# Two blocks of a transformer on one core: the low part of the logits' moving side, on 64 rows and padded to 128

## The chip, the cores and the metric

The kernel runs as one program on one core of one Trainium2 chip. The metric is the device time of an execution in microseconds (us); the figure for a kernel is the median over its runs. Five engines of the core matter here: PE multiplies matrices (and loads the stationary side of each product, listed as PEld), DVE, ACT and POOL work on elements, and SP issues the transfers.

## The reference, cut to what matters

512 tokens of 1024 features pass through two layers of a first block and two layers of a second block, each block with a mixing part and feed-forward parts. The mixing parts hold the heads of 64 features that this case is about:

```python
# first block: 6 attention heads and 6 retention heads of 64 features
scores = jnp.einsum('bnqhd,bnkhd->bnhqk', q, kb)      # + relative bias, softmax, times V
sc     = jnp.einsum('bnihd,bnjhd->bnhij', qc, kc)     # retention: decayed, causal, no softmax
# second block: stick-breaking heads, and 6 sparse-attention heads with two branches each
z  = jnp.einsum('bqhd,bkhd->bhqk', qb, k) * scale     # stick-breaking, 4 heads
ss = jnp.einsum('bqgrd,bgqnld->bgrqnl', qb, kg)       # selected keys
sw = jnp.einsum('bqgrd,bkgd->bgrqk', qb, kwb)         # window keys
```

All of these are products over 64 features. A further kind of head in the second block (MLA) has products over 96 features and is not touched.

## The kernel before, in words

Every large product is made of float parts: a number is split into a high part (rounded to the fast matmul type) and a low part (the rest), and a product is taken as high times high, low times high and high times low. For weights this is three passes per block of 128 x 128 (lines 529 to 531), each with a stationary load and a moving side of up to 512 tokens. The whole kernel is a stream of such passes, fed by weights that SP loads, ACT rounds (line 511) and DVE subtracts (line 513).

For the logits of a 64-feature head the three products fit into two passes, since the array has 128 rows. The stationary tile `st` holds the high part of a head in 64 rows and its low part in the other 64 (`still`). The moving tile `mh` holds the high part in both halves, so the first pass (line 616) gives high times high and low times high at once. The second pass (line 617) adds stationary high times moving low: only 64 rows have something to add, and it uses 64 rows of the stationary tile and 64 rows of `ml`. One tile `ml` holds the low parts of both heads of a pair, each in its own half.

`movings` makes these tiles: ACT writes the high part into one half, ACT or DVE copies it into the other, DVE writes the low part. It is called for retention queries (`rq`) and attention keys (`ak`) in the first block, three pairs each, and for stick-breaking queries (two pairs) and the keys `ks` and `kw` in the second: 20 times in all over two layers of each block. `qk` is called four times per head and branch, on 128, 256, 384 and 512 columns (tiles of queries against the keys up to them, or the reverse): 56 heads and branches, so 224 calls. The softmax (lines 714 to 726), transposes (line 744) and the product with the values (`pv`, line 776, 64 columns of the array per head) follow.

The order of the work is set in two steps: hand-written lists of jobs (`ORDER1`, `ORDER2`, `LAGS`) interleave heads with projections, and a scheduler then orders the instructions of each engine and gives tiles slots from pools. The pool `s` has 50 slots of 128 x 512; `mh`, `ml` and `st` come from it. Each engine runs its list strictly in order.

Of the kernel before, what the change touches and what calls it, by code (L numbers as in the profile page):

```python
# [11 lines left out]
F32 = mybir.dt.float32  # L12
# [7 lines left out]
T = 512  # L20
# [23 lines left out]
# stages for which a job of a kind waits before its next one  # L44
# [5 lines left out]
# the engine of each kind of copy, by phase  # L50
# [5 lines left out]
# taps of the convolution between two stages of its job  # L56
CONV_STEP = 2
# tiles of the first products by halves of the tokens, in block 1's FFN and in the FFN that follows block 1
HEAD1 = 4
HEAD2 = 2  # L60
# how the end of a phase is woven into the next products
# [6 lines left out]
# ---------------------------------------------------------------- host layout  # L68
# [44 lines left out]
class Plan:  # L113
    """Weights in chunks of at most 1024 columns of 128 rows, and the order in which the program takes them."""
# [18 lines left out]
class Blank:  # L133
    """Stands for the program's objects where only the order of the weights is asked for."""
# [14 lines left out]
# the jobs of each kind, in their order  # L149
# [13 lines left out]
# the order of the jobs of the two mixing phases; each advances those ahead of it by a stage  # L163
# [132 lines left out]
def _bias_master(rel_bias):  # L296
    """[layer, head, 128 queries, 512 keys] of the last query tile; keys of a later chunk are masked."""
    p = np.arange(128)[:, None]
    c = np.arange(512)[None, :]
    idx = np.clip(p + 384 - c, -128, 128) + 128  # L300
    m = rel_bias[:, :, idx]
    m[:, :, np.broadcast_to((c >= 448) & (p < 64), idx.shape)] = NEG
    return np.ascontiguousarray(m.astype(np.float32, copy=False))
# [48 lines left out]
# ---------------------------------------------------------------- the program  # L352
# [3 lines left out]
class Normed:  # L356
    """An input that awaits its norm's factor: the gained input in two parts, and the factor once known, as a row on
    all partitions and by token."""
# [6 lines left out]
class Prog:  # L365
# [23 lines left out]
    def phase(self, name, **bufs):  # L389
        """Pools of one phase: slots of [128, 512], long tiles of [128, 1280], values by token."""  # L390
        es = ExitStack()
        self.pools = {t: es.enter_context(self.tc.tile_pool(name=self.nm(name + t), bufs=b)) for t, b in bufs.items()}
        return es
# [41 lines left out]
    def pf(self, w=512):  # L435
        """Banks of every kind in turn, where no attention runs."""
        turns = "".join(t * b for t, b in BANKS.items())
        self.turn = (self.turn + 1) % len(turns)
        return self.bank(turns[self.turn], w)

    # ---- constants
    def consts(self):
        nc, A = self.nc, self.A

        def c(nm, shape, dt=F32):
            return self.cst.tile(shape, dt, tag=nm, name=nm)

        self.ident = c("ident", [128, 128])
        make_identity(nc, self.ident)
        self.ones = {}  # L450
        for d in (1024, 256, 128):
            self.ones[d] = c(f"ones{d}", [128, 1])
            nc.vector.memset(self.ones[d], 1.0 / d)
        self.one1 = c("one1", [128, 1])
        nc.vector.memset(self.one1, 1.0)
        self.m256 = c("m256", [128, 128])
        nc.vector.memset(self.m256, 1.0 / 256)
        self.m64 = c("m64", [128, 128])
        nc.vector.memset(self.m64, 0.0)
        nc.vector.memset(self.m64[0:64, 0:64], 1.0 / 64)  # L460
        nc.vector.memset(self.m64[64:128, 64:128], 1.0 / 64)
        self.tri = c("tri", [128, 128], F32R)
        nc.gpsimd.memset(self.tri.bitcast(F32), -1.0)
        nc.gpsimd.affine_select(self.tri, self.tri, pattern=[[-1, 128]], compare_op=ALU.is_ge,
                                fill=0.0, base=0, channel_multiplier=1)
        self.neg1 = c("neg1", [128, 128], F32R)
        nc.gpsimd.memset(self.neg1.bitcast(F32), -1.0)
        self.identr = c("identr", [128, 128], F32R)
        nc.vector.tensor_copy(self.identr, self.ident)
        self.smask = c("smask", [128, 128], F32R)  # L470
        nc.gpsimd.memset(self.smask.bitcast(F32), NEG)
        nc.gpsimd.affine_select(self.smask, self.smask, pattern=[[-1, 128]], compare_op=ALU.is_ge,
                                fill=0.0, base=0, channel_multiplier=1)
        # the first use of ScalarE loads its table while the first transfers are under way
        nc.scalar.activation(c("warm", [128, 1]), self.one1, AF.Copy)
        self.vec = c("vec", [128, NVEC])
        nc.sync.dma_start(self.vec, A["vec"])
        self.cmpv = c("cmpv", [128, 4])
# [9 lines left out]
    # ---- weights  # L488
# [11 lines left out]
    def fetch(self, end):  # L500
        """Loads and splits the chunks of the sequence before the given place."""
# [36 lines left out]
    def lin_tok(self, name, l, hd, width, tt, banks, sink):  # L538
        """Products by token, for the 128-token tiles tt; returns what hands them on."""
        mm = self.nc.tensor.matmul  # L540
        ps = {t: b(width) for t, b in zip(tt, banks)}
        for k in range(KD):
            wh, wl = self.blk((name, l, k))
            for t in tt:
                s = slice(128 * t, 128 * t + 128)
                mm(ps[t], hd.hi[k][:, s], wh, start=k == 0, stop=False)
                mm(ps[t], hd.lo[k][:, s], wh, start=False, stop=False)
                mm(ps[t], hd.hi[k][:, s], wl, start=False, stop=k == KD - 1)
            self.step()

        def end():
            for t in tt:
                sink(t, ps[t], hd.rt[:, t:t + 1])
        return end
# [6 lines left out]
    def open_mix(self, tok, names, l, hd, sink, halves):  # L561
        """The first products of a mixing phase, if so by halves of the tokens: values by token, two linear tiles."""
# [22 lines left out]
    # ---- splitting  # L585
# [15 lines left out]
    def movings(self, src, scale=None):  # L601
        """For the moving side, of both 64-row halves: [hi; hi], and lo in the rows that hold it."""
        lo, out = self.R("ml"), []
        for half in range(2):
            a, b = slice(64 * half, 64 * half + 64), slice(64 - 64 * half, 128 - 64 * half)
            m = self.R("mh")
# [3 lines left out]
            out.append((m, lo, a))  # L610
        return out

    def qk(self, ps, st, mv, c, stop=True):
        """ps = the product of a stationary [hi; lo] tile's columns and a moving side's columns c."""
        m, lo, a = mv
        self.nc.tensor.matmul(ps, st, m[:, c], start=True, stop=False)
        self.nc.tensor.matmul(ps, st[a], lo[a, c], start=False, stop=stop)  # L617

    def still(self, src, half, scale=None):
        """[hi; lo] of 64 rows for the stationary side."""  # L620
# [6 lines left out]
    # ---- norms  # L627
    def rstd(self, pc, n):
        """(pc + eps) ** -0.5 on [128, n]: Newton's steps from an estimate by the exponent's bits."""
# [12 lines left out]
    def bcast_rows(self, y, nt, g, bank=None):  # L642
        """y [128 tokens, nt * g] to a PSUM tile [128 = (g rows), nt * 128 tokens]."""
# [11 lines left out]
    def mean_rstd(self, accs, d, t0=0, t1=512, bank=None):  # L655
        """The norm's factor by token from squares in one or more tiles."""
# [40 lines left out]
    # ---- softmax attention over keys <= the end of the query tile  # L697
    def softmax(self, scores, master, gate=None, negated=True):
        """scores(qt, ps) emits the products, of the negated logits if so; yields, then normalises and transposes."""
# [33 lines left out]
    def key_parts(self, t):  # L733
        """A long tile as four key tiles, each with the queries from its own on."""
# [15 lines left out]
    def pipeline(self, jobs):  # L750
        """Each job's first stage follows one stage more of each of the jobs under way."""
# [19 lines left out]
    def pv(self, po, v, o, pts, start=True, stop=True):  # L771
        """po[:, q] += V^T P^T of two heads side by side in the array; their values are columns o on of v."""
# [6 lines left out]
    # ---- block 1  # L779
# [180 lines left out]
    def tail(self, keys_of, rh, rl, sink, done, halves):  # L960
        """The last products of a phase, if so by halves of the tokens."""
# [11 lines left out]
    def step(self):  # L973
        """A stage more of the end of a phase, whose stages are woven into the next products."""
        next(self.pending, None)

    def drain(self):
        """The rest of these stages; the norm's factor, if any, then takes their place."""
# [4 lines left out]
    def post_norm1(self, xs, f, g_post, g_next):  # L983
        """The sink and the end of a tail in block 1, and the next input."""
# [59 lines left out]
    def ffn(self, parts, head, names, l, hd, evict, partial):  # L1044
        """Up and down products part by part, the first ones by halves; returns what the tail takes."""
# [74 lines left out]
    # ---- block 2  # L1120
# [165 lines left out]
    def misc(self, l, hd, cx):  # L1286
# [6 lines left out]
        # the rotated key that all heads share  # L1293
# [4 lines left out]
        # gates by token  # L1298
# [77 lines left out]
    def nsa_in(self, l, hd, nx, nm, p=None):  # L1376
        """A linear tile, rotated but for the compressed values."""
# [27 lines left out]
        else:  # L1405
            # [128 = (token, token + 16) of 64 features, part, group, token]; the positions' part in the last 16 columns
# [38 lines left out]
    def compressed(self, l, nx, nm):  # L1445
        """Compressed keys (for both sides of the split) or values (block-diagonal by group)."""
# [4 lines left out]
        if nm == "k":  # L1451
# [8 lines left out]
            # columns by group, part and block  # L1460
# [4 lines left out]
        else:  # L1465
            # [128 = (copy, group, block), 64]
# [13 lines left out]
    def compressed_attention(self, nx, cx):  # L1480
        """All heads of two query tiles at a time; columns by pair, group and block."""
# [129 lines left out]
```

## Time and profile before

| | |
|---|---|
| runs | 3394.7, 3396.48 and 3407.11 us, median 3396.48 |
| profiled execution | span 3401.8 us (the page gives no other time of it) |
| PE busy | 3329.6 us, 98% |
| DVE / ACT / POOL busy | 1948.0 (57%) / 1349.7 (40%) / 258.7 us (8%) |
| first block's mixing parts | about 50 to 250 us and 690 to 900 us |
| second block's mixing parts | about 1650 to 1950 us and 2700 to 3000 us |

The busy time of PE includes the time in which a matmul is still in the pipeline, so two matmuls that follow each other overlap in the list. What a pass costs the stream is read from the distance between its start and the start of the next one. A stationary load is listed under PEld with its own start.

### The profile page before, as it was taken

The numbers are of one execution on the slowest core, as the hardware profiler recorded it, in microseconds if no ns is written. First come the engines' busy times: TensorE is split into PE (matmuls) and PEld (weight loads), VectorE is DVE, ScalarE is ACT, GpSimd is POOL, SyncE is SP. The second block draws the span as 40 slices with busy tenths as digits, with TensorE's granted clock in tenths as the row PEclk, the third lists the DMA queues.
The fourth block names the chain that finished last, engine by engine and source line by source line (L and its number), as shares of the span: only waits on it lengthen the run. The fifth ranks groups of instructions, "written<-read, shape, count | busy, mean of one in ns | idle before, by whom it ended". The sixth has DMA issues, their size and how long they took to land. (4 is left out here: it accounts for less than half of the span.)

```text
span 3401.8 us, 41132 instructions
## 1 busy us (share of the span) xinstructions
PE 3329.6 (98%) x15956; PEld 2697.0 (79%) x15956; DVE 1948.0 (57%) x3381; ACT 1349.7 (40%) x2254; POOL 258.7 (8%) x301
## 2 busy tenths in 40 slices
PE   8999999899999999999999999999999999999998
PEld 6778888877888888888877578888888877678887
DVE  5967334778744457454677564545445468554454
ACT  4364323435543333232566632223222366642231
POOL 2102000220200020000200010001000120010001
PEclk9999999999999999999999999999999999999999
DMA  5222222332132222232333022222222323112222
GB/s 166 89 70 81 97 96 99 112 121 85 57 112 96 97 93 98 95 99 95 114 86 112 13 94 99 99 93 95 98 99 93 118 81 106 52 62 99 95 97 69
DMA packets 100867, 317.28 MB, mean 93 GB/s; under 512 B 12608, under 2 KB 18112, under 8 KB 100672
## 3 DMA queue, kind: packets, MB, share of 16 engines
q1 hardware_dynamic: 100672, 314.66, 28.0%
q8 instruction: 125, 2.05, 0.2%
q14 instruction: 70, 0.57, 0.1%
HBM read 298.75 MB, written 6.29 MB: 90 GB/s over the span
## 5 line engine op out<-in xcount | busy, mean ns | idle before, releaser
L511 ACT ACTIVATE wh<-raw 128x1024 fp32r<-128x1024 f32 (+2 forms) x546 | 567.8, 1041 | 1411.6 <-PE pd L530 618.6
L513 DVE TENSOR_TENSOR wl<-raw,wh 128x1024 fp32r<-128x1024 f32 (+2 forms) x546 | 663.0, 1216 | 440.5 <-ACT wh L511 439.0
L529 PE MATMUL pd<-hh,wh 128*128 128x512 f32 (+1 forms) x1328 | 509.7, 386 | 3.7 <-ACT wh L511 3.7
L530 PE MATMUL pd<-hl,wh 128*128 128x512 f32 (+1 forms) x1328 | 509.3, 384 | 3.3 <-DVE hl L681 3.1
L531 PE MATMUL pd<-hh,wl 128*128 128x512 f32 (+1 forms) x1328 | 508.9, 384 | 2.1 <-DVE wl L513 2.1
L676 POOL TENSOR_TENSOR acc<-acc,sq 128x256 f32<-128x256 f32 (+1 forms) x160 | 172.4, 1081 | 2195.9 <-ACT sq L675 2190.6
L529 PEld LDWEIGHTS pd<-hh,wh 128*128 128x128 f32 x1328 | 251.1, 190 | 56.9 <-issue 6.7
L530 PEld LDWEIGHTS pd<-hl,wh 128*128 128x128 f32 x1328 | 252.4, 190 | 51.6 <-DVE hl L681 4.9
L531 PEld LDWEIGHTS pd<-hh,wl 128*128 128x128 f32 x1328 | 252.1, 190 | 49.6 <-DVE wl L513 2.5
L530 PE MATMUL pt<-hl,wh 128*128 128x512 f32 x480 | 189.7, 396 | 8.2 <-DVE hl L681 8.2
L530 PE MATMUL ps<-hl,wh 128*128 128x512 f32 (+1 forms) x528 | 196.8, 373 | 0.0
L529 PE MATMUL ps<-hh,wh 128*128 128x512 f32 (+1 forms) x528 | 196.5, 372 | 0.0
L531 PE MATMUL ps<-hh,wl 128*128 128x512 f32 (+1 forms) x528 | 196.3, 373 | 0.0
L531 PE MATMUL pt<-hh,wl 128*128 128x512 f32 x480 | 189.2, 395 | 0.0
L529 PE MATMUL pt<-hh,wh 128*128 128x512 f32 x480 | 188.6, 394 | 0.0
L529 PE MATMUL pd<-ah,wh 128*128 128x512 f32 (+1 forms) x498 | 185.0, 372 | 0.0
L530 PE MATMUL pd<-al,wh 128*128 128x512 f32 (+1 forms) x498 | 184.8, 371 | 0.0
L531 PE MATMUL pd<-ah,wl 128*128 128x512 f32 (+1 forms) x498 | 184.8, 371 | 0.0
L720 ACT ACTIVATE P<-P,st 128x128 f32<-128x128 f32 x192 | 107.0, 558 | 54.7 <-DVE st L714 44.1
L587 ACT ACTIVATE ah<-sc 128x512 fp32r<-128x512 f32 x88 | 55.6, 632 | 183.7 <-DVE sc L1129 183.7
L529 PE MATMUL pt<-ah,wh 128*128 128x512 f32 (+1 forms) x332 | 123.5, 372 | 0.0
L530 PE MATMUL ps<-al,wh 128*128 128x512 f32 (+1 forms) x332 | 123.4, 372 | 0.0
(475 smaller groups left out, 6510.9 us busy)
## 6 DMA issues: line engine op xcount, KB each, us to landing
raw<-in_w SPq DMA_DIRECT2D x514, 512.0 KB
raw<-in_w SPq DMA_DIRECT2D x20, 384.0 KB
xd<-x SPq DMA_DIRECT2D x16, 256.0 KB
x<-xd SPq DMA_DIRECT2D x16, 256.0 KB
sw<-sc SPq DMA_DIRECT2D x48, 64.0 KB
ct<-in_ret SPq DMA_DIRECT2D x12, 256.0 KB
sn<-in_ret SPq DMA_DIRECT2D x12, 256.0 KB
mst<-in_bias SPq DMA_DIRECT2D x12, 256.0 KB
```

What stands on the lines that cost most here:

```text
L511: nc.scalar.activation(h[:, :n], raw[:, :n], AF.Copy)
L513: eng.tensor_tensor(lo[:, :n], raw[:, :n], h[:, :n].bitcast(F32), op=ALU.subtract)
L529: mm(ps, h, rh[j][:, t0:t1], start=first and j == 0, stop=False)
L530: mm(ps, h, rl[j][:, t0:t1], start=False, stop=False)
L531: mm(ps, lo, rh[j][:, t0:t1], start=False, stop=last and j == n - 1)
L587: self.nc.scalar.activation(dst, src, AF.Copy, scale=scale)
L676: (eng or nc.gpsimd).tensor_tensor(acc, acc, w, op=ALU.add)
L720: nc.scalar.activation(p[:, :n], p[:, :n], AF.Exp, bias=m, scale=-1.0 if negated else 1.0, accum_out=st[:, 4 + qt:5 + qt])
```

## The change

`movings` now makes one low tile `ml` per head instead of one per pair. POOL sets the 64 rows of it that hold nothing to zero, and DVE writes the low part into the other 64 as before. `qk` multiplies the whole stationary tile with the whole low tile: 128 rows, of which 64 add zero. Number, columns and order of the arithmetic are otherwise as before. The diff also blanks comments and docstrings, so later lines move by two: 616 and 617 become 618 and 619.

```diff
     def movings(self, src, scale=None):
-        lo, out = self.R("ml"), []
+        out = []
         for half in range(2):
             a, b = slice(64 * half, 64 * half + 64), slice(64 - 64 * half, 128 - 64 * half)
-            m = self.R("mh")
+            m, lo = self.R("mh"), self.R("ml")
+            self.nc.gpsimd.memset(lo[b].bitcast(F32), 0.0)
             self.hi(m[a], src[a], 1.0 if scale is None else scale)
             self.copy("mh", m[b], src[a], scale)
             self.lo(lo[a], src[a], m[a], scale)
-            out.append((m, lo, a))
+            out.append((m, lo))
         return out
 
     def qk(self, ps, st, mv, c, stop=True):
-        m, lo, a = mv
+        m, lo = mv
         self.nc.tensor.matmul(ps, st, m[:, c], start=True, stop=False)
-        self.nc.tensor.matmul(ps, st[a], lo[a, c], start=False, stop=stop)
+        self.nc.tensor.matmul(ps, st, lo[:, c], start=False, stop=stop)
```

On POOL, at the start of the first mixing part (`sw` are tiles of the rotation, `st` retention's products, `ml` the low tiles), the order before is this:

```order
L802 TENSOR_TENSOR sw_438<-sw_438,sn_440 128x512
L802 TENSOR_TENSOR sw_449<-sw_449,sn_451 128x512
L824 AFFINE_SELECT st_514<-st_514 128x128 x4
L802 TENSOR_TENSOR sw_566<-sw_566,sn_568 128x512
L824 AFFINE_SELECT st_707<-st_707 128x128
L802 TENSOR_TENSOR sw_608<-sw_608,sn_610 128x512
L824 AFFINE_SELECT st_707<-st_707 128x128 x3
L824 AFFINE_SELECT st_726<-st_726 128x128 x4
```

And this is the same place in the changed kernel:

```order
L804 TENSOR_TENSOR sw_438<-sw_438,sn_440 128x512
L607 MEMSET ml_506 64x512
L804 TENSOR_TENSOR sw_449<-sw_449,sn_451 128x512
L607 MEMSET ml_512 64x512
L826 AFFINE_SELECT st_517<-st_517 128x128 x4
L804 TENSOR_TENSOR sw_569<-sw_569,sn_571 128x512
L826 AFFINE_SELECT st_713<-st_713 128x128 x2
L607 MEMSET ml_624 64x512
L607 MEMSET ml_630 64x512
L826 AFFINE_SELECT st_713<-st_713 128x128 x2
L804 TENSOR_TENSOR sw_611<-sw_611,sn_613 128x512
```

The memsets, 40 over the program, stand between the steps of the rotation and the causal masks of retention; a pair of them now stands inside a group of four masks.

On PE, in the first sparse-attention heads of the second block (`ps` logits, `po` the output, `pd` an output projection), the order before is this:

```order
L616 MATMUL ps_15392<-mh_14250,st_13739 128x128
L617 MATMUL ps_15392<-ml_14249,st_13739 128x128
L616 MATMUL ps_15401<-mh_14250,st_13739 128x384
L617 MATMUL ps_15401<-ml_14249,st_13739 128x384
L1546 MATMUL po_15564<-cp_15205,vc_15230 128x512
L616 MATMUL ps_15392<-mh_14250,st_13739 128x256
L617 MATMUL ps_15392<-ml_14249,st_13739 128x256
L616 MATMUL ps_15406<-mh_14250,st_13739 128x512
L617 MATMUL ps_15406<-ml_14249,st_13739 128x512
L529 MATMUL pd_15597<-msh_13925,wh_15296 128x512
```

And the changed kernel has this there:

```order
L618 MATMUL ps_15440<-mh_14291,st_13781 128x128
L619 MATMUL ps_15440<-ml_14292,st_13781 128x128
L618 MATMUL ps_15449<-mh_14291,st_13781 128x384
L619 MATMUL ps_15449<-ml_14292,st_13781 128x384
L1548 MATMUL po_15612<-cp_15253,vc_15278 128x512
L618 MATMUL ps_15440<-mh_14291,st_13781 128x256
L619 MATMUL ps_15440<-ml_14292,st_13781 128x256
L618 MATMUL ps_15454<-mh_14291,st_13781 128x512
L619 MATMUL ps_15454<-ml_14292,st_13781 128x512
L529 MATMUL pd_15645<-msh_13967,wh_15344 128x512
```

Nothing moved on PE here; the passes stand where they stood, and only the rows that the second pass uses differ. Elsewhere PE, DVE and ACT show small exchanges of neighbours.

## Rows read from the trace of the kernel before

**Rows 1.** The page's first lines: span; busy time, share and instructions by engine.

```profile
span 3401.8 us, 41132 instructions
PE 3329.6 (98%) x15956; PEld 2697.0 (79%) x15956; DVE 1948.0 (57%) x3381; ACT 1349.7 (40%) x2254; POOL 258.7 (8%) x301
```

**Rows 2.** Busy time by stretch: PE, PEld, DVE, ACT, POOL, clock, DMA.

```profile
100.00:200.00 100.00, 99.36 (x471) 75.46 (x470) 92.65 (x194) 45.80 (x79) 8.97 (x11) 1.00 0.27 86
350.00:450.00 100.00, 100.00 (x442) 82.78 (x442) 35.90 (x38) 35.62 (x46) 0.00 (x0) 1.00 0.28 95
1850.00:1950.00 100.00, 100.00 (x462) 61.20 (x461) 53.23 (x170) 62.78 (x156) 0.00 (x0) 1.00 0.09 31
```

**Rows 3.** Second passes on one bank, line 617: count, duration min/median/max, first and last start.

```profile
L617 PE MATMUL ps<-ml,st x208: 322/434/579, 64.4 to 2993.3; 64*128 64x256 f32 x48, 64*128 64x128 f32 x40, 64*128 64x512 f32 x12, 64*128 64x384 f32 x4
```

**Rows 4.** PE in order of time, sparse attention: start, duration, rows*columns of the array.

```profile
1894.91 0.40 PE L616 MATMUL ps<-mh,st 128*128 128x512 f32 x1
1895.23 0.50 PE L617 MATMUL ps<-ml,st 64*128 64x512 f32 x1
1895.66 0.51 PE L529 MATMUL pd<-msh,wh 128*128 128x512 f32 x1
1896.01 0.40 PE L530 MATMUL pd<-msl,wh 128*128 128x512 f32 x1
1896.24 0.22 PE L616 MATMUL ps<-mh,st 128*128 128x128 f32 x1
1896.39 0.33 PE L617 MATMUL ps<-ml,st 64*128 64x128 f32 x1
1896.64 0.50 PE L531 MATMUL pd<-msh,wl 128*128 128x512 f32 x1
1896.99 0.34 PE L616 MATMUL ps<-mh,st 128*128 128x384 f32 x1
1897.26 0.44 PE L617 MATMUL ps<-ml,st 64*128 64x384 f32 x1
1897.62 0.50 PE L529 MATMUL pd<-mmh,wh 128*128 128x512 f32 x1
1897.96 1.02 PE L1546 MATMUL po<-cp,vc 128*128 128x512 f32 x2
...
1899.03 0.38 PE L617 MATMUL ps<-ml,st 64*128 64x256 f32 x1
1899.34 0.49 PE L616 MATMUL ps<-mh,st 128*128 128x512 f32 x1
1899.76 0.49 PE L617 MATMUL ps<-ml,st 64*128 64x512 f32 x1
1900.18 0.64 PE L776 MATMUL po<-pt,v 128*64 128x512 f32 x1
```

**Rows 5.** The stationary loads of the same passes, with the idle time before them.

```profile
1894.68 0.19 PEld L616 LDWEIGHTS ps<-mh,st 128*128 128x128 f32 x1
1895.23 0.18 PEld L617 LDWEIGHTS ps<-ml,st 64*128 64x128 f32 x1 [0.36 <-issue]
1895.66 0.19 PEld L529 LDWEIGHTS pd<-msh,wh 128*128 128x128 f32 x1 [0.25 <-issue]
```

**Rows 6.** PE in order of time, MLA logits over 96 features.

```profile
1822.66 0.28 PE L1366 MATMUL ps<-kh,ql 96*128 96x256 f32 x1
1822.78 0.40 PE L531 MATMUL pd<-hh,wl 128*128 128x512 f32 x1
...
1823.25 0.39 PE L530 MATMUL pd<-hl,wh 128*128 128x512 f32 x1
1823.48 0.39 PE L1364 MATMUL ps<-kh,qh 96*128 96x512 f32 x1
1823.71 0.39 PE L1365 MATMUL ps<-kl,qh 96*128 96x512 f32 x1
```

**Rows 7.** A memset on POOL, by line: count, busy us, mean ns, idle before.

```profile
L1472 POOL MEMSET vc<- 128x512 f32 x2 | 1.1, 526 | 24.8 <-DVE ml L591 24.8
```

## The prediction, made before the changed kernel was run

> **What bounds the kernel now.** I read the page's totals first. PE is busy for 98% of the span of 3401.8 us, DVE for 57%, ACT for 40%, POOL for 8% [rows 1]. So the time is PE's stream, and the question is whether a pass of that stream costs more than its columns. The stretches come next: feed-forward work (350 to 450 us), the first block's mixing (100 to 200 us) and sparse attention (1850 to 1950 us) all show PE busy for 99 or 100 of 100 us at a granted clock of 1.00, the higher level of 2.4 GHz [rows 2]. But sparse attention loads stationary tiles for 61 us only where feed-forward work loads for 83 us [rows 2]: the list calls PE busy there, and less flows through it. So I went to the single passes in order of time and read the distance from one start to the next.
>
> Among plain passes a 512-column one takes 0.23 us (1896.01 to 1896.24) [rows 4]. Around the 64-row passes of line 617 it is otherwise. The 512-column case: from the first pass at 1894.91 to the second 0.32 us, from there to the next full pass 0.43 us, and that full pass, 512 columns too, takes 0.35 us [rows 4]. The three would take 0.69 us and take 1.10 us. The loads say why: a stationary load for a full pass starts with the pass ahead of it (1894.68, a pass early), while the load for the 64-row pass starts only at 1895.23, together with its own pass, after 0.36 us of idle time, and the load of the full pass behind it does the same after 0.25 us [rows 5]. So PE neither preloads into the 64-row shape nor out of it. It is not the zero work that costs: passes over 96 rows between full ones, in MLA, run at 0.12 us for 256 columns and 0.23 us for 512, entry (1823.25 to 1823.48) and exit included [rows 6].
>
> **What the change removes.** The second passes become full ones in their old places: PE's order is the same there. The extra time of one pass, its two neighbours included, by width:
> - 512 columns: 1.10 - 0.69 = 0.41 us, as above.
> - 384: from 1896.99 to 1897.96 (384, 384, 512 columns) 0.97 us. With 0.175 for 384, half way between 0.12 and 0.23, this would be 0.58, so 0.39 us extra [rows 4, 6].
> - 256: from 1899.03 to 1899.76 (256, 512) 0.73 us instead of 0.35: 0.38 us [rows 4, 6].
> - 128: from 1896.24 to 1896.99 (128, 128, 512) 0.75 us. A 128-column pass costs at most the 0.12 us of a 256-column one, so at least 0.28 us is extra [rows 4, 6].
>
> The mean is 0.365 us. There are 224 such passes, 56 of each width (208 of them on one bank [rows 3], 16 more on another, as the code has it). 224 x 0.365 = 82 us. Where the next pass is a product with the values on 64 columns, as at 1900.18 [rows 4], one switch stays: I take the entry cost of 0.32 - 0.23 = 0.09 us for 36 passes, counted in PE's order, 3 us. That leaves 79 us that PE's stream can lose. The bounds of this term: nothing, if the shape is not the reason, and 82 us.
>
> What comes back as waits, once PE needs less:
> - First block, 48 passes or 17.5 us per layer in some 180 us. In the stretch with the convolution DVE is busy for 92.65 of 100 us [rows 2], so no more than 7.35 us per 100 us can go there, against the 10 us that an even spread would take away. I let 4 us per layer be lost, 8 in all; bounds 0 and the whole 10 per layer.
> - Sparse attention, 48 passes or 17.5 us per layer. ACT is busy for 62.78 us and DVE for 53.23 us of 100 [rows 2]; of 82.5 us that is 76% and 65%, each at the end of a chain logits, minimum, exponential, transposes. I let 3.2 us per layer be lost, 6.5 in all; bounds 0 and half of the gain, 9 per layer.
> - Stick-breaking, 16 passes or 6 us per layer: nothing lost.
>
> **What it adds.** 40 memsets on POOL. The nearest row is 526 ns for 128 x 512 [rows 7]; 40 x 0.526 = 21 us on an engine that is idle for 92% of the span [rows 1]. Hidden, unless it is late: PE's first second pass of a head now waits for POOL as well, and behind it waits all of PE's stream. POOL is in order, and behind a memset stand the causal masks of retention and of stick-breaking, for which the products with the values wait. A memset waits for a free slot, and 20 more tiles ask for the same 50 slots. The nearest row is a memset that idled for 24.8 us in two places, 12.4 us each, until a slot was given back [rows 7]. Bounds: 0, and 20 x 12.4 = 248 us if every pair were held that long with PE behind it. I take 0, since `mh` of the same head asks for a slot of the same pool at the same point before and after, so most of that wait is there already; it cannot gain. DVE, ACT and SP get no instruction more or less; the exchanges of neighbours on them I cost at 0, within 3 us either way.
>
> A pass on half the rows could also run beside a neighbour on the other half, and padding would give that up. The rows show none of this: after the 512-column 64-row pass the next start is 0.43 us away [rows 4]. The Trainium skill, in "TensorE: Matmul & The Clock Gate", Part 3 on packing small matmuls, says that products in different row groups run side by side, a few ns apart. By that rule the 64-row shape would be worth keeping; the trace does not agree here, since every neighbour takes all rows or the same ones.
>
> **The sum.** 3401.8 - 79 + 8 + 6.5 = 3337 us on the profiled execution. Its span stands 5.3 us above the median of the runs, 3396.48, which is within the runs' own spread (to 3407.11); the page gives no time around the span, so I carry the difference over: 3332 us.
>
> **The rivals.**
> 1. All of it is had. Speaks for it: PE waits for hardly anything in these stretches, and the order is the same. Against: DVE at 92.65 of 100 [rows 2]. 3396.5 - 79 = 3317 us.
> 2. Another engine becomes the bound, so that about half is given back: the upper bounds of the waits, 10 and 9 us per layer, 38 us in all. For it: DVE's share with the convolution, and in-order chains. Against: ACT and DVE at a half to two thirds in sparse attention [rows 2]. 3396.5 - 79 + 38 = 3355 us.
> 3. Slower: the memsets hold POOL, in the mixing parts, at the 20 pairs. Each pair that holds up a mask or a first pass by w costs PE w. At the 12.4 us of rows 7 for half of the pairs it is 124 us, less 79: 3441 us. It makes the kernel slower than before from a mean of 79 / 20 = 4 us per pair on. For it: one pair stands inside a group of four masks in the new order. Against: POOL's idleness and the shared slot wait.
> 4. The change does not do what it says: the late load has another reason, such as two passes into one bank, and stays. Then 3396 us. Against: MLA's three passes into one bank do not show it [rows 6].
> 5. Padding gives up passes that ran side by side: each would then cost its own width, 0.12, 0.12, 0.175 and 0.23, mean 0.16 us; 224 x 0.16 = 36 us slower, 3432 us. Against: the 0.43 us above.
>
> **How the numbers follow.** Forecast 0.52, rival 1 0.15, rival 2 0.20, rival 3 0.06, rival 4 0.05, rival 5 0.02. About 0.5%, 17 us, is what a measurement of this kernel can tell from no change. Forecast, rivals 1 and 2 all lie beyond it: faster 0.87. Rival 4, and a part of rival 3 that just cancels the gain, make 0.07 for the same; slower 0.06. The range holds rival 1 with some room for the mean extra time (0.40 us instead of 0.365 would be 8 us more) and reaches past rival 2: 3307 to 3374. The forecast's own range is 3320 to 3345.
>
> **What would show it.** Right: the second passes (now line 619) start 0.12 to 0.23 us after the first ones and are followed after as long, their loads start with the pass ahead, and PE's loads in sparse attention take a larger share of a shorter stretch; about 17 us per layer go between the first and last logits of sparse attention. Wrong: the 0.4 us around a second pass stays (rival 4), POOL shows memsets with idle times of 5 us or more and PE waits for them (rival 3), or PE's waits for DVE in the convolution's stretch grow by as much as the passes gain (rival 2).

## The result, and the profile after

The changed kernel takes 3349.97 us (median of 4 runs, 3348.55 to 3351.22) against 3399.79 us before in the same comparison (3394.7 to 3407.11): a ratio of 0.9849, 95% interval 0.9834 to 0.9864. It is faster by 50 us. The forecast was 3332 us, with a range of 3307 to 3374; its direction and mechanism held, and it asked for 65 us on the profiled execution where 55 came.

The page's first lines after, which answer to [rows 1]:

```profile
span 3346.8 us, 41207 instructions
PE 3261.0 (97%) x15956; PEld 2678.4 (80%) x15956; DVE 1949.7 (58%) x3381; ACT 1343.6 (40%) x2254; POOL 284.3 (8%) x341
```

PE's busy time fell by 68.6 us, the span by 55.0. POOL has 40 instructions more, the memsets, and is busy for 25.6 us more; the memsets themselves are 21.0 of these (their line stands further down).

The single passes come first. PE in order of time in the changed kernel, at the place of [rows 4] (start, duration, pass):

```profile
1862.12 0.40 PE L618 MATMUL ps<-mh,st 128*128 128x512 f32 x1
1862.36 0.39 PE L619 MATMUL ps<-ml,st 128*128 128x512 f32 x1
1862.59 0.40 PE L529 MATMUL pd<-msh,wh 128*128 128x512 f32 x1
1862.82 0.39 PE L530 MATMUL pd<-msl,wh 128*128 128x512 f32 x1
1863.05 0.22 PE L618 MATMUL ps<-mh,st 128*128 128x128 f32 x1
1863.11 0.28 PE L619 MATMUL ps<-ml,st 128*128 128x128 f32 x1
1863.22 0.44 PE L531 MATMUL pd<-msh,wl 128*128 128x512 f32 x1
1863.54 0.45 PE L618 MATMUL ps<-mh,st 128*128 128x384 f32 x1
1863.82 0.34 PE L619 MATMUL ps<-ml,st 128*128 128x384 f32 x1
1864.00 0.39 PE L529 MATMUL pd<-mmh,wh 128*128 128x512 f32 x1
1864.23 1.10 PE L1548 MATMUL po<-cp,vc 128*128 128x512 f32 x2
```

The 512-column three (1862.12 to 1862.82) now take 0.70 us instead of 1.10: 0.40 less, where the prediction had 0.41. The second pass of 128 columns is followed after 0.11 us instead of 0.25, and the 128-column three (1863.05 to 1863.54) take 0.49 where 0.47 was reckoned. But the 384-column three (1863.54 to 1864.23) take 0.69 where 0.58 was reckoned. The loads of the same passes, which answer to [rows 5], say why:

```profile
1862.12 0.19 PEld L619 LDWEIGHTS ps<-ml,st 128*128 128x128 f32 x1
1862.36 0.19 PEld L529 LDWEIGHTS pd<-msh,wh 128*128 128x128 f32 x1
...
1863.16 0.19 PEld L531 LDWEIGHTS pd<-msh,wl 128*128 128x128 f32 x1
1863.54 0.19 PEld L618 LDWEIGHTS ps<-mh,st 128*128 128x128 f32 x1 [0.19 <-DVE st L716]
```

The load for the second pass starts with the pass ahead of it (1862.12), as for any full pass. The load of the next first pass, at 1863.54, has a new wait of 0.19 us: for the softmax minimum on DVE (line 716), which reads a logits bank empty. What the shape held back is now held back, in part, by the banks.

That holds for the whole program. Idle time of PE's loads by what ended it, the lines on the logits' passes that matter here, before (us in total, times, longest):

```profile
PEld ps L617 <- issue: 35.4, 138, 0.6
PEld ps L616 <- issue: 9.6, 34, 0.8
PEld ps L616 <- DVE st L714: 1.2, 2, 0.6
```

And after, two lines further down in the code:

```profile
PEld ps L619 <- issue: 1.7, 6, 0.4
PEld ps L618 <- issue: 3.9, 11, 0.8
PEld ps L618 <- DVE st L716: 4.4, 16, 0.6
PEld ps L618 <- ACT st L579: 3.8, 9, 1.0
PEld ps L618 <- DVE st L719: 2.6, 8, 0.5
```

"Issue" (nothing that the profile shows) fell from 45.0 to 5.6 us. The waits for the engines that empty the logits banks (the minimum, the maximum and the copy of retention's products) rose from 2.4 us (1.2, 0.4 and 0.8) to 10.8 (4.4, 2.6 and 3.8).

By stage, before (length, then busy us of PE, PEld, DVE, ACT and POOL, granted clock, share and GB/s of the transfers): the first block's mixing in its two layers, the second block's front half (stick-breaking and MLA) and its sparse attention, in both layers:

```profile
64.10:264.80 200.70, 200.07 (x972) 150.37 (x971) 153.01 (x335) 97.29 (x181) 24.51 (x37) 0.98 0.25 82
695.60:906.70 211.10, 208.94 (x1055) 159.14 (x1053) 165.89 (x360) 106.14 (x196) 31.58 (x41) 1.00 0.26 84
1634.50:1857.10 222.60, 217.05 (x1152) 172.42 (x1151) 161.56 (x340) 130.69 (x268) 26.03 (x37) 0.98 0.32 100
1857.10:1944.00 86.90, 86.90 (x386) 50.66 (x385) 48.28 (x164) 58.13 (x148) 0.00 (x0) 1.00 0.08 25
2689.60:2916.80 227.20, 219.35 (x1166) 172.91 (x1165) 167.31 (x349) 133.37 (x275) 26.68 (x37) 0.99 0.32 100
2916.80:3002.20 85.40, 85.40 (x390) 49.81 (x389) 46.01 (x158) 56.21 (x143) 0.00 (x0) 1.00 0.06 19
sum 1033.90, PE 1017.71 PEld 755.31 DVE 742.07 ACT 581.82 POOL 108.80; mean PE 169.62 PEld 125.89 DVE 123.68 ACT 96.97 POOL 18.13
```

The same stretches after, between the same passes:

```profile
63.80:249.80 186.00, 183.29 (x972) 145.28 (x971) 153.07 (x335) 95.65 (x181) 30.44 (x47) 1.00 0.27 88
680.50:878.60 198.10, 194.27 (x1055) 156.17 (x1053) 166.22 (x360) 104.34 (x196) 37.46 (x51) 1.00 0.27 90
1606.40:1830.60 224.20, 212.13 (x1151) 169.35 (x1150) 167.00 (x341) 131.56 (x269) 32.53 (x45) 0.99 0.31 100
1830.60:1903.80 73.20, 72.88 (x385) 47.95 (x385) 47.10 (x165) 56.78 (x148) 0.00 (x0) 1.00 0.08 30
2647.20:2874.70 227.50, 216.56 (x1166) 173.33 (x1165) 164.88 (x346) 131.90 (x271) 32.40 (x44) 0.98 0.31 99
2874.70:2947.70 73.00, 72.68 (x389) 47.15 (x388) 45.75 (x161) 55.31 (x145) 0.00 (x0) 1.00 0.07 23
sum 982.00, PE 951.81 PEld 739.23 DVE 744.03 ACT 575.53 POOL 132.82; mean PE 158.64 PEld 123.21 DVE 124.00 ACT 95.92 POOL 22.14
```

The sums: length -51.9 us, PE busy -65.9, so PE's idle time (length less busy) +14.0, from 16.2 to 30.2. The first block gains 14.7 and 13.0 us, sparse attention 13.7 and 12.4. The front half of the second block loses 1.6 and 0.3 us: its PE is busy for 4.9 and 2.8 us less, and idle for 6.5 and 3.1 us more. That is the place where the forecast failed, and most of the experiments are about it.

One caution goes with every such comparison. The stretches were not all granted the full clock. Length times (1 - granted clock), added up, is some 11 us in the rows before and 7 in those after: an estimate, worked out from these rows, of what the lower clock cost (the last section shows 18 passes in 7 us at 0.52 and 34 at 1.00, so passes slow down with it). So about 4 of the 51.9 and 65.9 us may be the clock's, and a step of a few us in one stretch of one execution is read beside its clock.

### The profile page after: what moved, and what is told of

It is laid out like the page before. It is cut to its first block, busy times and chain, and to the rows that moved or that the text cites. A ratio compares the mean times of both kernels' runs of the same rounds, so it can differ in the third digit from the quotient of the medians.

```text
span 3346.8 us, 41207 instructions
## 1 busy us (share of the span) xinstructions
PE 3261.0 (97%) x15956; PEld 2678.4 (80%) x15956; DVE 1949.7 (58%) x3381; ACT 1343.6 (40%) x2254; POOL 284.3 (8%) x341
## 5 line engine op out<-in xcount | busy, mean ns | idle before, releaser
L531 PE MATMUL ps<-ah,wl 128*128 128x512 f32 (+1 forms) x332 | 123.3, 371 | 0.0
```

The source lines that it names most:

```text
L531: mm(ps, lo, rh[j][:, t0:t1], start=False, stop=last and j == n - 1)
```

## The experiments

Theory L: behind stick-breaking's logits stands an in-order chain of ACT, DVE and POOL, and it, not PE, sets that stretch. Theory D: it is DVE's load there. Theory O, the first rival: only the order of the work there moved. In the changed kernel a weight's subtraction (1.2 us) went ahead of the low parts for which the first second pass waits. PE's order moved with it: the first second pass stands 1.8 us behind its first pass (1651.77 to 1653.59), and 0.9 us before (1677.42 to 1678.29). So the prediction's "PE's order is the same there" holds for sparse attention, and not here.

DVE in front of the first stick-breaking logits, before:

```profile
1676.86 0.42 DVE L583 TENSOR_SCALAR mh<-sc 64x512 fp32r<-64x512 f32 x1
1677.31 0.68 DVE L593 SCALAR_TENSOR_TENSOR ml<-sc,mh 64x512 fp32r<-64x512 f32 x1
1678.02 0.42 DVE L583 TENSOR_SCALAR mh<-sc 64x512 fp32r<-64x512 f32 x1
1678.47 0.69 DVE L593 SCALAR_TENSOR_TENSOR ml<-sc,mh 64x512 fp32r<-64x512 f32 x1
1679.20 1.23 DVE L513 TENSOR_TENSOR wl<-raw,wh 128x1024 fp32r<-128x1024 f32 x1
```

And after:

```profile
1650.71 0.88 DVE L583 TENSOR_SCALAR mh<-sc 64x512 fp32r<-64x512 f32 x2
1651.62 1.23 DVE L513 TENSOR_TENSOR wl<-raw,wh 128x1024 fp32r<-128x1024 f32 x1
1652.76 1.39 DVE L593 SCALAR_TENSOR_TENSOR ml<-sc,mh 64x512 fp32r<-64x512 f32 x2
```

**1. The order put back.** In stick-breaking the second head's copy is held until the first head's low part is issued:

```diff
-            self.copy("mh", m[b], src[a], scale)
+            if half and scale is not None:
+                with self.tc.issue_after(first.ins):
+                    self.copy("mh", m[b], src[a], scale)
...
+            first = self.lo(lo[a], src[a], m[a], scale)
```

> The changed kernel, with one ordering edge in the stick-breaking queries: on DVE the copy of the second head's high part comes after the first head's low part, as it did before. This puts DVE's order in that stage back (the weight split of 1.2 us stands behind the low parts again). Theory O (the stage's 6 us per layer were lost since the split moved ahead of the low parts): 12 us below the changed kernel's 3350, so about 3338. Theory L (the stage is set by its own chain of exponential, logarithm and splits, so shorter passes are worth nothing there): 3350, within 3 us. The POOL theory (memsets that come late): 3350, and PE waits for POOL in that stage.

Measured: 3350.26 us, ratio 0.9859 [0.9844, 0.9873], the same as the changed kernel. The front halves take 450.7 us together instead of 451.7. Theory O falls as the cause. So does the theory that the memsets come late: no wait of PE names one. PE's 15956 instructions and DVE's 3381 stand here in the very order of experiment 2's kernel, so these two differ in stick-breaking's rows and memsets and in next to nothing else.

**2. All padded but stick-breaking.** `movings` takes a switch; stick-breaking shares one `ml` and keeps its 64-row passes:

```diff
-        opened[nm] = ... else self.movings(ps, 0.125)
+        opened[nm] = ... else self.movings(ps, 0.125, False)
```

> Padding in retention, attention and sparse attention; the 16 stick-breaking passes per layer stay on 64 rows with one shared low tile, and the order there is that of before. If padding the stick-breaking heads brought nothing (O and L alike): 3350, within 3 us. If it did bring its 6 us per layer and something else took it back outside that stage: 3362.

Measured: 3351.72 us, ratio 0.9865 [0.9847, 0.9883]; the padding of stick-breaking's 32 passes brings 1.75 us, or 1.46 against experiment 1 with its equal order, both within the spread of the runs. The sum of the two front halves here:

```profile
sum 453.40, PE 437.05 PEld 346.78 DVE 327.74 ACT 262.86 POOL 58.59; mean PE 218.53 PEld 173.39 DVE 163.87 ACT 131.43 POOL 29.30
```

The changed kernel's two stretches, above, add up to 451.7 us with PE busy for 428.69. So the passes do get cheaper there (PE busy -8.4 us, of which 2 or 3 can be the clock's: 0.97 and 0.99 here, 0.99 and 0.98 in the changed kernel), and PE's idle time rises by 6.7 us, from 16.4 to 23.0. In experiment 1 it is 21.3.

**3. No second passes at all.** The product with the low moving part is left out at all 224 places, and the low tiles are as before. The edit is to the kernel before:

```diff
-        self.nc.tensor.matmul(ps, st, m[:, c], start=True, stop=False)
-        self.nc.tensor.matmul(ps, st[a], lo[a, c], start=False, stop=stop)
+        self.nc.tensor.matmul(ps, st, m[:, c], start=True, stop=stop)
```

> The kernel before without its 224 second passes: the products of high stationary and low moving parts of the 64-feature logits are left out. If PE's stream still sets the time, a padded pass costs its columns, mean 0.16 us: 3350 - 36 = 3314, and a 64-row pass cost (3400 - 3314) / 224 = 0.38 us. If after the change another engine sets the time (rival 2 of the prediction), leaving the passes out brings little more: 3340 to 3350.

Measured: 3333.56 us, ratio 0.9805 [0.979, 0.9819]. The passes that are left out are 33 us of columns by the pitches after (0.06, 0.12, 0.18 and 0.23 us, 56 of each), and 16.4 us come of it. In the six stretches PE's busy time falls by another 20.6 us (951.8 to 931.2) and its idle time rises by 5.2 (30.2 to 35.4). The granted clock can account for the rest. In the six stretches here it was 1.00, 1.00, 0.95, 0.98, 0.97 and 0.95, so length times (1 - granted clock) is some 23 us against 7 in the changed kernel: an estimate from the rows, 16 us, which is what is missing. All four runs show it, with 0.986 to 0.988 over the whole program against 0.990 to 0.992. By this estimate the padded passes cost about their columns, and PE's stream still sets most of the time.

**4. 96 rows instead of 128** for the first head of each pair: its second passes use rows 0 to 95, and 32 rows are set to zero:

```diff
-            self.nc.gpsimd.memset(lo[b].bitcast(F32), 0.0)
+            z, r = (slice(64, 96), slice(0, 96)) if half == 0 else (b, slice(0, 128))
+            self.nc.gpsimd.memset(lo[z].bitcast(F32), 0.0)
...
-        self.nc.tensor.matmul(ps, st, lo[:, c], start=False, stop=stop)
+        self.nc.tensor.matmul(ps, st[r], lo[r, c], start=False, stop=stop)
```

> The changed kernel, with the first head of each pair padded to 96 rows only (32 rows of zeros), the second to 128. If the extra time belongs to a switch into a shape of at most 64 rows, 96 rows pass like full ones: 3350, within 5 us. If any pass on fewer than 128 rows pays it, half of the gain is lost: 3375.

Measured: 3351.05 us, ratio 0.986 [0.9845, 0.9875], as with 128 rows. PE in this kernel:

```profile
1866.63 0.22 PE L619 MATMUL ps<-mh,st 128*128 128x128 f32 x1
1866.69 0.28 PE L620 MATMUL ps<-ml,st 96*128 96x128 f32 x1
1866.80 0.45 PE L531 MATMUL pd<-msh,wl 128*128 128x512 f32 x1
```

The pass over 96 rows starts 0.06 us after the full one and is followed after 0.11 us, as the full pass at 1863.11 above. What costs is the 64-row shape, not that rows are missing: 0.28 to 0.41 us per 64-row pass between full ones by the prediction's four cases, nothing for 96 rows. The Trainium skill, "TensorEngine Tiling (Array Packing)", Tiling Modes, says under Key Properties that a change of tiling mode drains the engine, and under Available Configurations it lists 64 rows among the modes and 96 not. The rows here agree in so far as the 64-row passes pay and those over 96 rows do not.

One more thing changed with the rows: a pair's two heads no longer share one low tile. No run keeps 64 rows with a tile for each head, so this is not separated by an edit. Against it speaks that the late loads waited for no other instruction that the profile shows. The products with the values, on 64 columns of the array, show the same kind of idle time with no tile of the change in them: 26.3 us for "issue" in front of their loads before, 26.4 after.

**5 and 6. The chain cut short.** In both, ACT's exponential and logarithm in stick-breaking's softplus are left out; the first keeps stick-breaking's 64-row passes (as experiment 2), the second pads them. The main lines of the edit:

```diff
-                nc.scalar.activation(e, e, AF.Exp, scale=-1.0)
-                nc.scalar.activation(e, e, AF.Ln, bias=self.one1)
```

> Left out in this kernel and the next: the exponential and the logarithm inside stick-breaking's softplus (ACT's two passes behind each absolute value), 32 ACT instructions per layer. Here stick-breaking keeps its 64-row passes; all other second passes are padded. Theory L (the chain of ACT, DVE and POOL behind stick-breaking's logits sets the time of that stretch, so PE's gain there turns into waits) and theory M (nothing is left to gain there because the 64-row passes of stick-breaking never cost their 0.37 us in the first place) both let this kernel be 0 to 25 us below 3352, since ACT and the chain lose work; this run is the base for the next.

> As the kernel before in this list, but stick-breaking's second passes are padded too. Theory L: with the chain shortened, the passes count again, 16 passes of 0.365 us per layer, 5.8 us, in two layers 12 us: this kernel is 8 to 12 us below the other one. Theory M, or a chain still bound by DVE and POOL behind ACT: the two differ by less than 3 us.

Measured: 3346.79 us (0.9844 [0.983, 0.9858]) and 3343.38 us (0.983 [0.9817, 0.9842]): 3.4 us apart, between the two expectations. In the front halves PE's busy time falls by 6.9 us (431.87 to 424.99) and its idle time rises by 4.1, less than the 6.7 of experiment 2 against the changed kernel. Theory L has a part in it, but not the whole; which part, the waits further down show. Theory M falls by single passes: on 384 columns, from the first pass to the one behind the second, stick-breaking takes 0.68 us before (1685.18, 1685.49, 1685.86) and 0.49 after (1660.22, 1660.44, 1660.71).

**7 and 8. The weights' subtraction on POOL** in the second block's mixing, in the changed kernel and in the kernel before:

```diff
-ENG2 = dict(..., wlo="v",
+ENG2 = dict(..., wlo="g",
```

> The changed kernel, with the subtraction that makes the low part of a weight (line 513 of before) done by POOL instead of DVE in the second block's mixing parts; nothing is left out. Theory D (DVE, which is busy for 73% of the stick-breaking stretch and 87% of the MLA stretch, sets the pace of the front half of the second block's mixing once the passes are cheap): these stretches get shorter by 3 to 8 us per layer, 3334 to 3344 us. Theory L alone (a chain of latencies, ACT's share included, not DVE's load): 3345 to 3355, or slower if POOL's longer subtraction is late for PE.

> The kernel before with the same subtraction on POOL. Theory D: without padding PE has less to wait for DVE, so this gains less than the changed kernel does from the same edit, 0 to 5 us, and the step from here to the padded kernel with it is 55 to 62 us instead of 50. Theory L alone: the step stays at 50 us, within 4.

Measured: 3404.02 us (1.0012 [1.0002, 1.0022]) and 3474.65 us (1.022 [1.0207, 1.0234]). The edit costs 54 us in the changed kernel and 76 in the kernel before. Theory D's times are missed by far, theory L allowed for a late POOL, and the step between the two, 71 us, is outside of both. POOL in the first of them, the full shape alone (count, busy us, mean ns, idle before):

```profile
L513 POOL TENSOR_TENSOR wl<-raw,wh 128x1024 fp32r<-128x1024 f32 x62 | 151.0, 2439 | 317.9 <-ACT wh L511 213.8 <-ACT P L722 50.0 <-PE ps L1368 25.5
```

That is 2.44 us where DVE takes 1.24 in the changed kernel. The clock fell too: the front halves were granted 0.93 and 0.93 in the first and 0.91 and 0.91 in the second, which by the same estimate is some 35 and 47 us, against 7 in each kernel without the edit. As a test of theory D the pair is spoilt, because it puts a slower engine in the way and comes with a lower clock. The next pair takes the load away without that.

**9 and 10. The subtraction left out** in the second block's mixing, with `lo = h` in its place:

```diff
...
-            eng.tensor_tensor(lo[:, :n], raw[:, :n], h[:, :n].bitcast(F32), op=ALU.subtract)
+            lo = h
+            if self.eng["wlo"] != "n":
+                lo = self.wp.tile([128, 1024], F32R, tag="wl", name=self.nm("wl"))
+                nc.vector.tensor_tensor(lo[:, :n], raw[:, :n], h[:, :n].bitcast(F32), op=ALU.subtract)
```

> Left out in this kernel and the next: the subtraction that makes the low part of a weight, in the second block's mixing parts alone; the passes that used the low part use the high part instead, so PE has the same passes, and DVE loses 74 instructions of 1.22 us, 90 us in all, with nothing put on another engine. This one is otherwise the kernel before. Theory D (DVE sets the pace of stick-breaking and MLA): 0 to 15 us below 3398, as PE's 64-row passes still fill part of the time. Theory L alone (latency of the chain, not DVE's load): within 4 of 3398.

> The changed kernel with the same subtraction left out. Theory D: with DVE relieved, the padding of stick-breaking pays: from the start of the second block's mixing to the start of sparse attention each layer gains 3 to 7 us over the kernel ahead of this one in the list (where before and after showed -1.7 and -0.3 us), and the step between the two kernels is 55 to 64 us. Theory L alone: that stretch gains less than 2 us per layer, and the step stays at 50, within 4.

Measured: 3395.59 us (0.9986 [0.9976, 0.9995]) and 3344.61 us (0.9838 [0.9824, 0.9852]). The step is 51 us, as without the edit, and the front halves show no gain (448.7 us, then 449.6; 4.0 us lost in one layer, 3.1 gained in the other). But they were granted 1.00 and 0.99 in the first and 0.98 and 0.98 in the second, some 5 to 7 us by the estimate above, so a gain of that size can be hidden there; the medians are what counts. DVE is busy there for 68 to 70 us less (331.89 to 264.05 us in the padded kernel), and little comes of it: the step stays at 51 and not at 55 to 64. DVE's load alone is not the bound. PE's idle time rises less: by 4.3 us through the padding (13.3 to 17.6), against 9.6 from before to after (13.4 to 23.0).

**11 and 12. Both cuts together**, with 64-row and with padded passes in stick-breaking, all others padded (the edits of 5 and 9, and of 6 and 10).

> Left out in this kernel and the next: both the softplus' exponential and logarithm in stick-breaking and, in the second block's mixing, the subtraction that makes a weight's low part. Here stick-breaking keeps its 64-row passes, all others are padded. Theory L + D (the wait that takes the gain is shared: the chain through ACT and DVE's load each hold PE for about half of it, 4 us each of the 9.6 us by which PE's idle time grew): this is the base. 3338 to 3347.

> As the kernel before in this list, with stick-breaking padded too. Theory L + D: with both relieved, PE's idle time in the two stretches from the start of the second block's mixing to sparse attention grows by less than 2 us in all through the padding, its busy time falls by 7 to 8, and this kernel is 5 to 8 us faster than the one before in the list. If neither is the cause (the waits come from the order on PE itself or from another engine's queue): idle time grows by 4 us or more again, and the two are within 4 us.

Measured: 3343.1 us (0.9832 [0.9818, 0.9845]) and 3337.59 us (0.9807 [0.9794, 0.9821]): 5.5 us apart, within the 5 to 8 that L and D together expected. The runs of 5 and 6 don't overlap, nor do those of 11 and 12; those of 2 and the changed kernel do. The two front halves with 64-row passes:

```profile
sum 446.50, PE 429.46 PEld 341.21 DVE 259.29 ACT 239.53 POOL 54.39; mean PE 214.73 PEld 170.60 DVE 129.65 ACT 119.76 POOL 27.20
```

and padded:

```profile
sum 445.80, PE 427.02 PEld 342.39 DVE 262.18 ACT 240.91 POOL 60.61; mean PE 213.51 PEld 171.20 DVE 131.09 ACT 120.46 POOL 30.30
```

PE's idle time rises by 1.7 us only (17.0 to 18.8), as expected. Its busy time falls by 2.4 and not by 7 to 8. The first of the two stretches was granted 0.98 in the padded profile and 1.00 in the other, some 4 us by the estimate above; without that the fall would be near 7.

The pairs that differ in stick-breaking's padding alone, in order:

| | idle time of PE through the padding | medians |
|---|---|---|
| nothing cut (2, changed kernel) | +6.7 us | -1.8 us |
| nothing cut, equal order (2, 1) | +5.0 us | -1.5 us |
| chain cut (5, 6) | +4.1 us | -3.4 us |
| chain and DVE's load cut (11, 12) | +1.7 us | -5.5 us |

The rows are in the order that theories L and D expect, but the medians of a few runs don't separate them (1.6 and 2.1 us from row to row), and the idle times are of single executions. The waits of PE in the two front halves say more (us, by what PE waited for):

| | 2 (64 rows) | 1 | changed | 5 (64 rows) | 6 | 9 (64 rows) | 10 | 11 (64 rows) | 12 |
|---|---|---|---|---|---|---|---|---|---|
| the softplus in two parts, `sp` | 0 | 0.8 | 3.0 | 0 | 0.4 | 0 | 0.8 | 0 | 0.4 |
| the high part of MLA's queries, `qh` | 3.0 | 4.6 | 4.0 | 0 | 0 | 0 | 0 | 0 | 0 |
| a norm's factor, `bt` | 0.4 | 3.0 | 3.0 | 0.4 | 3.0 | 0.4 | 3.0 | 0.4 | 3.0 |

The first is a wait for the work behind the logits, and the second for work on the same in-order engines. They grow with the padding (2 against 1 and the changed kernel). Leaving out the softplus leaves 0.4 us of them, leaving out DVE's subtraction 0.8. So this work does hold PE, but these runs don't divide its share between theories L and D: either one removes the wait for `qh`, and in 10 a wait of 4.5 us for DVE at another place (`gelu`, line 1436) is new. The third wait grows by 2.6 us in each pair, whatever is cut, and belongs to none of the theories: PE waits for a norm's factor at one place more, 0.7 us per layer, and 0.6 us longer at another. At the latter the memsets play a part:

```profile
1617.64 1.09 POOL L607 MEMSET ml<- 64x512 f32 x2
1618.22 0.54 DVE L637 TENSOR_SCALAR y<-y 128x4 int32<-128x4 int32 x1
```

While these memsets run, two small steps of the factor on DVE take 0.41 and 0.54 us; in experiment 2, without them, both take 0.17. It is the same in the other layer (0.41 and 0.54 at 2656).

Of the 4.1 us of experiments 5 and 6, 1.5 are a wait for DVE's `x` (line 1025) at the start of one stretch alone. The profiles of before, 1, 2 and the changed kernel have it in one stretch too and 5's in none, so it is not the padding's. No experiment that does the whole computation beats the changed kernel beyond the spread of the runs.

## Why the prediction was right, and where it missed

**The mechanism held.** The 64-row shape was the reason (rival 4 falls: the passes start 0.06 to 0.28 us after the first ones and their loads with the pass ahead), nothing ran side by side (rival 5), and the price per pass fits: 0.40 us at 512 columns against 0.41 forecast. POOL was hardly a hindrance (rival 3): nothing waits for a memset but one copy on ACT, once, for 3.8 us, and the factor of the norm above comes 0.6 us later per layer. The memsets after, to set beside [rows 7]:

```profile
L607 POOL MEMSET ml<- 64x512 f32 x40 | 21.0, 525 | 45.5 <-DVE ml L591 20.3 <-DVE y L856 13.7 <-DVE raw L1401 4.1
```

40 at 525 ns, 21 us, as reckoned; the long idle times stand where nobody waits.

**First block: right in size.** 17.5 less 4 per layer was expected, and 14.7 and 13.0 came. In the first of them some 3 us are the clock's: before had a stretch at the lower clock there (below).

**Sparse attention: right in sum.** 17.5 less 3.2 was expected, 13.7 and 12.4 came. PE is still busy for 72.9 of 73.2 us, so the return did not come as idle time. It sits in the loads: the waits of 0.2 us for a logits bank, shown above.

**Stick-breaking: the step that failed** is "16 passes or 6 us per layer: nothing lost". All was lost in the stretches, -1.6 and -0.3 us, and the medians of experiments 2 and 1 give 1.5 us of the 12. The step looked at PE alone, which is busy for 217 of 222.6 us there. A stretch can be full on PE and have other chains close behind it. That is what experiments 1, 2, 5 and 6 show: the passes got cheaper, and 5.0 to 6.7 us came back as waits, for the softplus and MLA's queries (all but 0.4 us gone when the softplus is cut) and for a norm's factor (there all the same).

**The 79 us were too many.** PE's busy time fell by 65.9 us in the stretches that hold all 224 passes, 0.29 us each and not 0.365. The price of a 64-row pass was right, as at 1862.12; what was wrong is how much of it would go. From the start of each first pass to its second, and from there to the next pass, the two traces add up to 145 us before and 90 after; their columns alone are 66 (0.06, 0.12, 0.18 and 0.23 us, twice, 56 of each). So 79 us stood above the columns before and 24 still do: there the load's head start runs into a bank that is not yet empty, or into another wait, which the list counts in part as busy PE. So the returns came in two forms: 14 us of idle PE, for which 14.5 had been allowed, and the load waits, which had not been allowed for.

The rest of the distance from 3332 to 3350 is in the base: the profile of before stands 2.0 us above the median of this comparison and that of after 3.2 below its own, so 55.0 us of span are 49.8 us of medians (the granted clock over the whole program was 0.989 in the one profile and 0.992 in the other); and the median of before came out at 3399.79 and not at 3396.48. The result lies 5 us above the forecast's own range (3320 to 3345) and 5 us below rival 2's 3355 us, so the number alone doesn't choose between them. But rival 2's reason (half given back on DVE with the convolution and in sparse attention) is not what happened there.

## What to carry to other kernels

A product over 64 rows in a stream of full passes can be dearer than the same product padded with zeros: read the distance between starts around it, and where its load begins, and not its columns. Price a removed stall only up to the next consumer: list, stage by stage, which bank or tile PE would wait for if it came 10% earlier, even where PE reads as 98% busy. Busy PE in the list includes waits of 0.1 to 0.3 us in front of a load, so look at PEld's releasers for returns that the busy share doesn't show. And before a cause is named, list PE's waits by what they wait for in both kernels, with the granted clock beside them.

## What the runs showed of the hardware

A pass over 96 rows costs no switch, one over 64 rows about 0.4 us with its neighbours (experiment 4). POOL takes 2.44 us for the subtraction of 128 x 1024 that takes DVE 1.24, and clears 64 x 512 in 0.525 us. Beside such a memset two small steps on DVE took 0.41 and 0.54 us instead of 0.17 each.

The clock was not the same everywhere. Before, from 65 to 72 us (length, PE busy, then as above):

```profile
65.00:72.00 7.00, 7.00 (x18) 5.01 (x18) 1.31 (x3) 0.96 (x2) 2.39 (x5) 0.52 0.60 174
```

After, in the same stretch:

```profile
65.00:72.00 7.00, 7.00 (x34) 5.75 (x33) 3.10 (x5) 1.55 (x3) 1.70 (x5) 1.00 0.54 153
```

0.52 is near the lower level of 1.2 GHz, 1.00 the higher of 2.4: 18 passes against 34 in 7 us. In both, PE had been idle for 1.32 us shortly ahead (63.38 us before, 63.09 after); what followed were 64-row passes before and full ones after. Experiment 9, with 64-row passes and 1.33 us of idle time there, was granted 0.53, and seven kernels padded there, with 1.31 or 1.32 us, all 1.00. But experiment 8, with 64-row passes and 1.20 us, was granted 1.00 too. No run varies the idle time and the passes apart, so the padding is not shown to be the reason, and the 3 us stay out of its account.
